# A fused QKV projection: Strassen on pairs of row tiles, and Hopcroft-Kerr on triples in its place

## The chip, the cores and the metric

The kernel runs on one core of a Trainium2 chip. The metric is the device time of one execution in microseconds (us); lower is better. A core has a matrix engine (TensorE, PE in the profile, its weight loads apart as PEld), three engines for elementwise work (VectorE or DVE, ScalarE or ACT, GpSimd or POOL) and queues that issue DMAs, here mostly that of SyncE (SP). Each engine works through its own queue in order; engines wait for each other through semaphores. Matmuls write PSUM, which has 8 banks of 512 f32 columns; all else lies in SBUF.

## The reference

```python
batch, seq, hidden = 16, 512, 768
qkv = np.matmul(x, w_qkv)            # (16, 512, 768) @ (768, 2304), f32
q, k, v = (qkv[..., n * hidden:(n + 1) * hidden] for n in range(3))
return np.stack([q, k, v], axis=0).astype(np.float32)
```

So it is one product of an 8192 x 768 matrix with a 768 x 2304 matrix, written as three outputs. In row tiles of 128 rows there are 64 tiles; the inner dimension is 6 chunks of 128.

## The kernel before

Everything is ordered by hand (`manual_schedule`, L57): each engine's queue is the order in which the program text issues its instructions. The inner dimension is cut into two halves of 3 chunks, and x is taken in pairs of row tiles (256 rows, 32 pairs). The 2304 columns are cut in two units `q` = 0, 1 of 2 x 512 columns and a remainder `REM` of 256 columns between them.

*Start.* The first three pairs are computed directly, in bf16, while the weights arrive. `load_rows` (DMA at L141) brings rows as they lie, `cast_rows` and `turn_rows` round and transpose them, the latter by TensorE transposes (L167) and copies from PSUM (L145, L147). `block` (L385) runs the chains of six matmuls of 512 columns, with copies out on ACT (L394). Meanwhile DVE casts weights and makes the weight sums of the fast scheme (`sum_w`, L113; a last cast L456), each a 128 x 1536 operation.

*Steady part.* Each of the other 29 pairs goes through `two` (the last through `last`). A pair and a unit are a 2 x 2 by 2 x 2 block product, done with 7 block products instead of 8 (`product`, L212: three matmuls of 512 columns each). Products 1 and 2 are bf16, the other five are f32r (recorded as f32), with operands that are sums. `do` issues one product and what follows it: a copy from a PSUM bank to the output tile by ACT (L226, L233, L239, L243) or an add of a bank to the output tile by DVE (L230, L240, L246; one operand in SBUF, one in PSUM). Sums that several outputs share are not formed anew: the next product accumulates in the same bank. The 256 remaining columns are done directly (`rem_row`, L262; copy L272).

*x for the next pair.* `load_x` (L126) loads x in four DMAs two pairs ahead, two issued by SP and two by ACT. `transpose` (L130, DVE) transposes 32 x 32 blocks of 128 x 1536. POOL rounds to bf16 (`round_x`, L175) and makes four sums and a copy (`sums_x`, L183 to L187; 128 x 384 each). `early` puts this behind the pair's first products.

*Stores.* `store_quad` (L253 to L258) issues on SP two stores per unit, of both row tiles at once, and `rem` one (L273).

The order of products in `two` is a1 b1, remainder, a2 b2 a6 b6 a5 a7 b5 b7 a4 a3 b4 b3, 42 matmuls of 512 columns and 12 of 256 per pair.

Of the kernel before, what the change touches and what calls it, by code (L numbers as in the profile page):

```python
# [10 lines left out]
def kernel(  # L11
# [19 lines left out]

# [3 lines left out]
    B, T, H = x.shape  # L35
    M = B * T
# [5 lines left out]
    NP = M // (2 * P)  # L42
    CB = 512
    REM = N3 - 4 * CB
    Q_OFF = (0, 2 * CB + REM)
    R_OFF = 2 * CB
# [5 lines left out]
    sub = mybir.AluOpType.subtract  # L52

    x_flat = x.rearrange("b t h -> (b t) h")
    out_flat = out.rearrange("s b t h -> s (b t) h")

    ctx.enter_context(tc.manual_schedule())  # L57

    w_pool = ctx.enter_context(tc.tile_pool(name="w", bufs=1))
    tq_pool = ctx.enter_context(tc.tile_pool(name="tq", bufs=2))  # L60
    bt_pool = ctx.enter_context(tc.tile_pool(name="bt", bufs=1))
    o_pool = ctx.enter_context(tc.tile_pool(name="o", bufs=5))
    st_pool = ctx.enter_context(tc.tile_pool(name="st", bufs=4))
    or_pool = ctx.enter_context(tc.tile_pool(name="or", bufs=2))
    xin_pool = ctx.enter_context(tc.tile_pool(name="xin", bufs=3))
    xf_pool = ctx.enter_context(tc.tile_pool(name="xf", bufs=2))
    xb_pool = ctx.enter_context(tc.tile_pool(name="xb", bufs=4))
    rem_pool = ctx.enter_context(tc.tile_pool(name="rem", bufs=1))
    s_pool = ctx.enter_context(tc.tile_pool(name="s", bufs=2))
    ps_pool = ctx.enter_context(tc.tile_pool(name="ps", bufs=8, space=bass.MemoryType.PSUM))  # L70

    tiny = w_pool.tile([P, 1], fp32, name="tiny")
    eye = w_pool.tile([P, 176], bf16, name="eye")[:, :P]
    w_rem = [w_pool.tile([P, KH, REM], bf16, name="w_rem0"), None]

    b1 = [w_pool.tile([P, KT, CB], bf16, name=f"b1_{q}") for q in range(2)]
    b22 = [w_pool.tile([P, KH, CB], f32r, name=f"b22_{q}") for q in range(2)]
    t_0 = w_pool.tile([P, 4, KH, CB], f32r, name="t_0")  # L80
    w_rem[1] = rem_pool.tile([P, KH, REM], bf16, name="w_rem1")
    ts = [[t_0[:, n] for n in range(4)], None]

    def load_w(dst, j0, nj, off, cols):
        rows = w_qkv.rearrange("(p j) n -> p j n", j=KT)
        nc.sync.dma_start(dst, rows[:, j0:j0 + nj, off:off + cols])

    stage = {}

    def load_blocks(q, c, nj=KH):
        if q == 0:
            t = tq_pool.tile([P, KT, CB], fp32, name="st0", tag="tq")
            for j in range(0, KT, nj):
                load_w(t[:, j:j + nj], j, nj, Q_OFF[q] + c * CB, CB)
            stage[q, 0, c], stage[q, 1, c] = t[:, :KH, :], t[:, KH:, :]
        else:
            for h in range(2):  # L100
                t = st_pool.tile([P, KH, CB], fp32, name="st1", tag="st")
                load_w(t[:], h * KH, KH, Q_OFF[q] + c * CB, CB)
                stage[q, h, c] = t[:]

    def sum_w(q, n):
        t1, t2, t3, t4 = ts[q]
        o, in0, in1 = {
            1: (t1, stage[q, 0, 1], stage[q, 0, 0]),
            2: (t2, stage[q, 1, 1], t1),
            3: (t3, stage[q, 1, 1], stage[q, 0, 1]),  # L110
            4: (t4, stage[q, 1, 0], t2),
        }[n]
        nc.vector.tensor_tensor(o, in0, in1, op=sub)  # L113

    xin, xf, xb, sr = {}, {}, {}, {}

    def load_x(p, other):
        xin[p] = xin_pool.tile([P, 2 * P // G, KC], fp32, name="xin")  # L120
        t = xin[p]
        rows = x_flat[p * 2 * P:(p + 1) * 2 * P, :].rearrange("(g b) k -> b g k", b=G)
        for n in range(2):
            for h in range(2):
                i = 2 * h + n
                (nc.sync, other)[h].dma_start(t[i * G:(i + 1) * G], rows[:, :, i * KC:(i + 1) * KC])  # L126

    def transpose(p):
        t = xf_pool.tile([P, KT, 2 * P], fp32, name="xf")
        nc.vector.transpose(  # L130
            t[:].rearrange("p j (g b) -> p g j b", b=G),
            xin.pop(p)[:].rearrange("p g (a j) -> p g j a", a=G),
        )
        xf[p] = t

    def load_rows(p):
        xin[p] = xin_pool.tile([P, 2, K], fp32, name="xin")
        rows = x_flat[p * 2 * P:(p + 1) * 2 * P, :]  # L140
        nc.sync.dma_start(xin[p][:], rows.rearrange("(r m) k -> m r k", m=P))  # L141

    def copy_halves(dst, src, two):

        nc.vector.tensor_copy(out=dst[0], in_=src[0])  # L145
        if two:
            nc.scalar.activation(dst[1], src[1], ident)  # L147
        else:
            nc.vector.tensor_copy(out=dst[1], in_=src[1])

    xc = {}

    def cast_rows(p, two=True):
        src = xin.pop(p)
        xc[p] = s_pool.tile([P, 2, K], bf16, name="xc", tag="s")
        for r in range(2):
            halves = (slice(0, K // 2), slice(K // 2, K))
            copy_halves([xc[p][:, r, n] for n in halves], [src[:, r, n] for n in halves], two)

    def turn_rows(p, two=True):  # L160
        c = xc.pop(p)
        xb[p] = xb_pool.tile([P, KT, 2 * P], bf16, name="xb", tag="xb")
        for r in range(2):
            cols = c[:, r, :].rearrange("m (p j) -> m j p", j=KT)
            ps = ps_pool.tile([P, KT, P], bf16, name="ps")
            for j in range(KT):
                nc.tensor.transpose(ps[:, j, :], cols[:, j, :], eye)  # L167
            ks = (slice(0, KH), slice(KH, KT))
            copy_halves(
                [xb[p][:, n, r * P:(r + 1) * P] for n in ks], [ps[:, n, :] for n in ks], two  # L170
            )

    def round_x(p):
        xb[p] = xb_pool.tile([P, KT, 2 * P], bf16, name="xb", tag="xb")
        nc.gpsimd.tensor_copy(out=xb[p][:], in_=xf[p][:])  # L175

    def sums_x(p):
        t = xf.pop(p)
        a11, a12 = t[:, :KH, :P], t[:, KH:, :P]
        a21, a22 = t[:, :KH, P:], t[:, KH:, P:]  # L180
        s = s_pool.tile([P, 5, KH, P], f32r, name="s")
        g = nc.gpsimd
        g.tensor_tensor(s[:, 1], a21, a22, op=add)  # L183
        g.tensor_tensor(s[:, 2], s[:, 1], a11, op=sub)  # L184
        g.tensor_tensor(s[:, 3], a11, a21, op=sub)  # L185
        g.tensor_copy(out=s[:, 0], in_=a22)
        g.tensor_tensor(s[:, 4], a12, s[:, 2], op=sub)  # L187
        sr[p] = s


    class Quad:
        pass

    def quad(p, q):
        u = Quad()
        u.p, u.q = p, q
        u.o = o_pool.tile([P, 2, 2 * CB], fp32, name="o", tag="o")
        u.x = u.y = u.z = None
        return u

    def product(u, n, ps, start):
        t1, t2, t3, t4 = ts[u.q]
        if n <= 2:
            h = (n - 1) * KH
            lhs = [xb[u.p][:, h + j, :P] for j in range(KH)]
            rhs = [b1[u.q][:, h + j, :] for j in range(KH)]
        else:
            k, t = {3: (4, b22[u.q][:]), 4: (0, t4), 5: (1, t1), 6: (2, t2), 7: (3, t3)}[n]
            lhs = [sr[u.p][:, k, j, :] for j in range(KH)]
            rhs = [t[:, j, :] for j in range(KH)]  # L210
        for j in range(KH):
            nc.tensor.matmul(  # L212
                ps[:], lhs[j], rhs[j],
                start=(start and j == 0), stop=(j == KH - 1), skip_group_check=True,
            )

    def bank():
        return ps_pool.tile([P, CB], fp32, name="ps")

    def do(u, n):  # L220
        c11, c12 = u.o[:, 0, :CB], u.o[:, 0, CB:]
        c21, c22 = u.o[:, 1, :CB], u.o[:, 1, CB:]
        if n == 1:
            u.x = bank()
            product(u, 1, u.x, True)
            nc.scalar.activation(c11, u.x[:], ident)  # L226
        elif n == 2:
            u.z = bank()
            product(u, 2, u.z, True)
            nc.vector.tensor_tensor(c11, c11, u.z[:], op=add)  # L230
        elif n == 6:
            product(u, 6, u.x, False)
            nc.scalar.activation(c12, u.x[:], ident)  # L233
        elif n == 5:
            u.y = bank()
            product(u, 5, u.y, True)
        elif n == 7:
            product(u, 7, u.x, False)
            nc.scalar.activation(c22, u.x[:], ident)  # L239
            nc.vector.tensor_tensor(c22, c22, u.y[:], op=add)  # L240
        elif n == 4:
# [182 lines left out]
    for j in range(2, KT):  # L424
        cast_k(j)
# [75 lines left out]
```

## Time and profile before

| what | value |
|---|---|
| timed runs, median (lowest to highest of 3) | 363.17 us (363.01 to 363.24) |
| profiled execution, span from first to last instruction | 361.3 us |
| TensorE matmul | 353.4 us busy, 1765 recorded |
| TensorE weight load | 251.0 us busy |
| DVE | 224.4 us busy |
| ACT | 182.9 us busy |
| POOL | 173.9 us busy |
| DMA | 108.08 MB, 299 GB/s on average; SP's queue 80.8%, ACT's 9.6% of the 16 engines' time |
| granted TensorE clock | 1.000 |

The page gives no other time of the profiled execution than its span; the timed runs are other executions of the same program, 1.8 us longer than the span. Busy time of TensorE is not a rate: the records of successive matmuls overlap, so the distance between their starts is what one costs. The same holds for DVE and ACT where nothing is waited for: the next instruction starts about 0.08 (DVE) or 0.10 us (ACT) before the record of the one ahead of it ends. A line such as `L240 DVE TENSOR_TENSOR o<-o,ps 128x512 f32 ... x58 | 39.9, 688 | 91.2 <-ACT` names the source line, the engine, the tiles written and read, their shape, the count, the busy us in all, the mean ns of one, and the idle us ahead of it with what ended the wait.

### The profile page before, as it was taken

The page shows a single profiled execution, that of the slowest core. Times are in us where ns is not written, and L with a number is a line of the kernel's source. Part 1 is how long each engine was busy: PE and PEld are TensorE (multiplying, and loading weights), DVE is VectorE, ACT ScalarE, POOL GpSimd, SP SyncE. Part 2 cuts the span into 40 slices and gives each one's busy share as a digit, 9 for nine tenths or more (in the row PEclk, how much of TensorE's full clock was granted, in tenths as well). Part 3 has the DMA queues.
Part 4 walks back from the last instruction along what each step waited for, and adds up shares of the span by engine and source line. Part 5 has one row for each costly group of instructions (what it writes and reads, how often), then busy time and mean ns, then how long its engine had stood idle before and what let it go on. Part 6 is the DMA issues. An engine that isn't in the chain of part 4 may idle for free.

```text
span 361.3 us, 5221 instructions
## 1 busy us (share of the span) xinstructions
PE 353.4 (98%) x1765; PEld 251.0 (69%) x1797; DVE 224.4 (62%) x239; ACT 182.9 (51%) x304; POOL 173.9 (48%) x180
## 2 busy tenths in 40 slices
PE   8999999999999999999999999999999999999995
PEld 3644577777777777777777777777777777777763
DVE  3499826765566765566675565676556676556642
ACT  4547555455454545454545445455545454545452
POOL 0001861746664445664445665444665444666410
PEclk9999999999999999999999999999999999999999
DMA  7999869988898999899899999998989899999666
GB/s 298 405 388 373 286 221 359 331 289 295 278 328 301 294 273 294 276 324 315 280 280 290 281 308 309 291 289 278 292 288 321 295 300 271 297 272 339 264 261 232
DMA packets 80617, 108.08 MB, mean 299 GB/s; under 512 B 4816, under 2 KB 60368, under 8 KB 80592
## 3 DMA queue, kind: packets, MB, share of 16 engines
q1 hardware_dynamic: 65184, 96.35, 80.8%
q10 hardware_dynamic: 15408, 11.41, 9.6%
q8 instruction: 14, 0.23, 0.3%
q14 instruction: 11, 0.09, 0.1%
HBM read 32.24 MB, written 75.50 MB: 298 GB/s over the span
## 4 chain that ended last, share of the span: by engine, by line
PE 96%; ACT 1%; issue 1%; ACTq 0%; DVE 0%
PE ps L212 75%; PE ps L262 11%; PE ps L385 9%; PE ps L365 1%; PE ps L167 1%; ACT o L243 0%; ACTq L303 0%; ACT xb L147 0%; ACT orem L317 0%; DVE xb L145 0%; ACT xc L147 0%; ACTq L319 0%; DVE zero L346 0%; ACTq L317 0%
## 5 line engine op out<-in xcount | busy, mean ns | idle before, releaser
L212 PE MATMUL ps<-t,s 128*128 128x512 f32 x696 | 173.8, 398 | 0.0
L212 PEld LDWEIGHTS ps<-t,s 128*128 128x128 f32 x696 | 130.7, 188 | 29.7
L175 POOL CAST xb<-xf 128x1536 bf16<-128x1536 f32 x29 | 43.8, 1510 | 168.3 <-DVE xf L130 156.0
L240 DVE TENSOR_TENSOR o<-o,ps 128x512 f32<-128x512 f32 x58 | 39.9, 688 | 91.2 <-ACT o L239 91.2
L130 DVE STREAM_TRANSPOSE xf<-xin 128x1536 f32<-128x1536 f32 x29 | 85.5, 2950 | 3.7 <-DMA out_dram<-orem 2.1
L212 PE MATMUL ps<-b,xb 128*128 128x512 bf16 x320 | 82.4, 380 | 1.5
L239 ACT ACTIVATE o<-ps 128x512 f32<-128x512 f32 x58 | 34.8, 600 | 44.2 <-PE ps L212 44.2
L212 PEld LDWEIGHTS <-xb 128*128 128x128 bf16 x348 | 31.7, 98 | 35.6 <-issue 7.3
L233 ACT ACTIVATE o<-ps 128x512 f32<-128x512 f32 x58 | 34.9, 601 | 42.1 <-PE ps L212 39.4
L246 DVE TENSOR_TENSOR o<-o,ps 128x512 f32<-128x512 f32 x58 | 39.9, 688 | 21.3 <-PE ps L212 20.2
L212 PE MATMUL ps<-b,s 128*128 128x512 f32 x174 | 48.7, 389 | 0.0
L262 PE MATMUL ps<-w_rem,xb 128*128 128x256 bf16 x384 | 47.2, 273 | 0.0
L243 ACT ACTIVATE o<-ps 128x512 f32<-128x512 f32 x58 | 34.7, 599 | 24.1 <-PE ps L212 21.3
L226 ACT ACTIVATE o<-ps 128x512 f32<-128x512 f32 x58 | 34.7, 598 | 23.8 <-DVE o L246 20.6
L262 PEld LDWEIGHTS <-xb 128*128 128x128 bf16 x384 | 37.4, 98 | 11.2 <-issue 0.5
L230 DVE TENSOR_TENSOR o<-o,ps 128x512 f32<-128x512 f32 x58 | 36.5, 673 | 5.4 <-PE ps L212 4.1
L212 PEld LDWEIGHTS ps<-b,s 128*128 128x128 f32 x174 | 32.7, 188 | 6.8
L184 POOL TENSOR_TENSOR s<-s,xf 128x384 fp32r<-128x384 f32 x29 | 30.0, 1035 | 2.3
L183 POOL TENSOR_TENSOR s<-xf 128x384 fp32r<-128x384 f32 x29 | 30.9, 1064 | 0.0
L185 POOL TENSOR_TENSOR s<-xf 128x384 fp32r<-128x384 f32 x29 | 29.5, 1017 | 0.0
L187 POOL TENSOR_TENSOR s<-xf,s 128x384 fp32r<-128x384 f32 x29 | 29.5, 1016 | 0.0
L272 ACT ACTIVATE orem<-ps 128x512 f32<-128x512 f32 x31 | 18.5, 598 | 20.7 <-PE ps L262 19.5
(36 smaller groups left out, 129.4 us busy)
## 6 DMA issues: line engine op xcount, KB each, us to landing
out_dram<-o SPq DMA_DIRECT2D x62, 768.0 KB, 4.8
out_dram<-o SPq DMA_DIRECT2D x65, 256.0 KB, 4.1
xin<-in_x_dram SPq DMA_DIRECT2D x62, 192.0 KB, 6.9
xin<-in_x_dram ACTq DMA_DIRECT2D x54, 192.0 KB, 4.4
out_dram<-orem SPq DMA_DIRECT2D x31, 256.0 KB, 5.7
st<-in_w_qkv_dram SPq DMA_DIRECT2D x6, 768.0 KB, 13.1
xin<-in_x_dram SPq DMA_DIRECT2D x3, 768.0 KB, 5.7
st<-in_w_qkv_dram SPq DMA_DIRECT2D x6, 256.0 KB, 6.1
```

Of the source, the lines that this page charges most:

```text
L130: nc.vector.transpose(t[:].rearrange("p j (g b) -> p g j b", b=G), xin.pop(p)[:].rearrange("p g (a j) -> p g j a", a=G),)
L175: nc.gpsimd.tensor_copy(out=xb[p][:], in_=xf[p][:])
L212: nc.tensor.matmul(ps[:], lhs[j], rhs[j], start=(start and j == 0), stop=(j == KH - 1), skip_group_check=True,)
L226: nc.scalar.activation(c11, u.x[:], ident)
L230: nc.vector.tensor_tensor(c11, c11, u.z[:], op=add)
L233: nc.scalar.activation(c12, u.x[:], ident)
L239: nc.scalar.activation(c22, u.x[:], ident)
L240: nc.vector.tensor_tensor(c22, c22, u.y[:], op=add)
L243: nc.scalar.activation(c21, u.x[:], ident)
L246: nc.vector.tensor_tensor(c12, c12, u.y[:], op=add)
L262: nc.tensor.matmul(ps, xb[p][:, j, r * P:(r + 1) * P], w_rem[j // KH][:, j % KH, :], start=(j == 0), stop=(j == KT - 1), skip_group_check= ...
L385: nc.tensor.matmul(ps[n][:], xb[p][:, j, r * P:(r + 1) * P], w[:, j, :], start=(j == 0), stop=(j == KT - 1), skip_group_check=True,)
```

## The change

The kernel is rewritten around triples of row tiles. Seven row tiles (`ND`) are computed directly in bf16, in groups of six matmuls of 384 columns (`HC`, half of q, k or v). The other 57 form 19 triples. Rows i = 1, 2, 3 of a triple have two halves of the inner dimension, x_i and y_i; the weights have the halves u_c and v_c for c = 1, 2, 3 (q, k, v). A triple times the weights is a 3 x 2 by 2 x 3 block product, done by 15 block products instead of 18, for each half of 384 columns (`Half`, `run`). A block product is three matmuls of 384 columns. 13 of the 15 are f32r with operands that are sums; C and C' are bf16.

Six PSUM banks (12, 31, 32, 23, 13, 21; 31 and 32 alternate between two banks each) hold running chains. A chain may be *seeded*: ACT or DVE writes its first value into PSUM and matmuls accumulate on top. Per half, ACT seeds 31 and 13 from ta (the copy of product A) and DVE seeds 21, 32 and 23 from ta, e12 and e31 (SBUF copies made by ACT). Three products of a half (N7, Q7, Q6) run within the next half.

x for the next triple: three block transposes on DVE (`first`, `between`), two roundings and two negations on ACT (`late_1`), eleven sums on POOL (four behind the third transpose, one in `late_1`, six at the triple's end). All loads and stores are issued by SP; a store is one row tile's 384 columns. Weight sums: M6 and M7 on POOL, A and B' on ACT, the others on DVE, in tiles of 128 x 2304. The core of the diff:

```diff
-    o_pool = ctx.enter_context(tc.tile_pool(name="o", bufs=5))
+    t_pool = ctx.enter_context(tc.tile_pool(name="t", bufs=13))
+    s_pool = ctx.enter_context(tc.tile_pool(name="s", bufs=16))
+    x_pool = ctx.enter_context(tc.tile_pool(name="x", bufs=8))
+    c_pool = ctx.enter_context(tc.tile_pool(name="c", bufs=15))
+    e_pool = ctx.enter_context(tc.tile_pool(name="e", bufs=5))
...
+        def sum_x(self, name):
+            (x1, y1), (x2, y2), (x3, y3) = (self.xy(i) for i in range(3))
+            s, g = s_tile(f32r), self.s
+            a, b, op = {
+                "A": lambda: (x1, y1, add),
+                "M1": lambda: (x2, y1, add),
+                "B'": lambda: (x2, y2, add),
+                "N1": lambda: (g["A"][:], x3, sub),
+                "Q1": lambda: (g["B'"][:], y3, sub),
+                "M6": lambda: (x1, x2, sub),
+                "M7": lambda: (y2, y1, sub),
+                "N6": lambda: (x3, x1, sub),
+                "N7": lambda: (y3, g["N1"][:], sub),
+                "Q7": lambda: (y3, y2, sub),
+                "Q6": lambda: (x3, g["Q1"][:], sub),
+            }[name]()
+            two(pool, s[:], a, b, op)
...
+        for j in range(KH):
+            pe.matmul(
+                ps[:, :HC], lhs[:, j, :], rhs[:, j0 + j, h * HC:(h + 1) * HC],
                 start=(start and j == 0), stop=(j == KH - 1), skip_group_check=True,
             )
...
+    def run(H_, prev, first, between, late):
+        u = H_.u
+        H_.mul("A", "12", True)
+        ta = e_tile()
+        H_.keep(ta[:], H_.read("12"))
+        first()
+        if prev:
+            prev.mul("N7", "31")
+            prev.mul("Q7", "23")
+        H_.keep(H_.read("31"), ta[:], -1.0)
+        H_.keep(H_.read("13"), ta[:])
+        if prev:
+            prev.end_31()
+        H_.mul("B", "12")
+        e12 = e_tile()
+        H_.keep(e12[:], H_.read("12"))
+        if prev:
+            prev.end_23()
+        two(dve, H_.read("21"), ta[:], e12[:], sub)
+        H_.mul("C", "31")
+        e31 = e_tile()
+        H_.keep(e31[:], H_.read("31"))
+        two(dve, H_.read("32"), e31[:], ta[:], add)
+        dve.scalar_tensor_tensor(H_.read("23"), e31[:], -1.0, e12[:], mult, sub)
+        H_.mul("A'", "13")
+        c11 = H_.take("13", 1, 1, -1.0)
+        if prev:
+            prev.mul("Q6", "32")
+            prev.end_32()
+        H_.mul("M1", "12")
+        c21 = c_tile()
+        two(dve, c21[:], c11[:], H_.read("12"), add)
+        between()
+        H_.mul("B'", "21")
+        c22 = H_.take("21", 2, 2, -1.0)
+        H_.mul("N1", "31")
+        late()
+        H_.mul("C'", "32")
+        c33 = H_.take("32", 3, 3, -1.0)
+        H_.mul("Q1", "23")
+        H_.c32 = c_tile()
+        two(dve, H_.c32[:], c22[:], H_.read("23"), add)
+        c13 = c_tile()
+        two(dve, c13[:], c33[:], H_.read("31"), add)
+        H_.mul("M6", "12")
+        H_.take("12", 1, 2)
+        H_.mul("M7", "21")
+        two(dve, c21[:], c21[:], H_.read("21"), add)
+        H_.out(2, 1, c21)
+        H_.mul("N6", "13")
+        two(dve, c13[:], c13[:], H_.read("13"), add)
+        H_.out(1, 3, c13)
...
+    sum_w("A'", dve, u1, v1, sub)
+    minus_w("A", u1)
+    for h in range(2):
+        for r in range(4, ND):
+            group(r, 0, h, wq)
+    for h, engines in ((0, (dve, act)), (1, (dve, dve))):
+        cut = slice(h * HC, (h + 1) * HC)
+        for k, (eng, t) in enumerate(zip(engines, (u2, v2))):
+            copy(eng, wk[:, k * KH:(k + 1) * KH, cut], t[:, :, cut])
+    sum_w("M6", pool, u1, u2, add)
+    sum_w("M7", pool, v1, v2, add)
+    sum_w("B", dve, u2, v2, sub)
+    sum_w("M1", dve, u1, v2, add)
...
+    sum_v3("N7", v1, v3, add)
+    transpose(ND)
+    transpose(ND + 1)
+    minus_w("B'", v2)
...
+    sum_w("Q6", dve, u3, u2, add)
+    sum_v3("N1", v3, T["A'"], sub)
+    transpose(ND + 2)
+    for name in ALL[:4]:
+        t0.sum_x(name)
...
+    sum_w("Q1", dve, u3, T["B"], add)
+    sum_w("N6", dve, T["N1"], u3, sub)
+    for r in range(ND):
+        group(r, 2, 0, wv)
+    sum_v3("Q7", T["Q1"], v3, sub)
...
+        def first_1():
+            if nxt:
+                transpose(r1 + 2)
+                for name in ALL[:4]:
+                    nxt.sum_x(name)
...
+        def late_1():
+            if nxt:
+                nxt.round_x("B")
+                nxt.round_x("A'")
+                nxt.sum_x("Q1")
+                nxt.minus_x(0)
+                nxt.minus_x(1)
+
+        half = Half(u, 0, n)
+        run(half, prev, first_0, between_0, late_0)
+        prev, n = half, n + 1
+        half = Half(u, 1, n)
+        run(half, prev, first_1, nothing, late_1)
+        prev, n = half, n + 1
+        if nxt:
+            for name in ALL[5:]:
+                nxt.sum_x(name)
+            nxt.drop()
```

`first_0` and `between_0` each transpose one row tile of the next triple. `two` is a tensor_tensor of the engine named; `keep` is an ACT copy with a scale, `take` an ACT copy into an output tile with its store, `end_31`, `end_23` and `end_32` finish an output of the half before.

## The prediction

> **What bounds the kernel now.** I read the busy shares, then the chain that ended last, then the timelines of single engines. All times are microseconds from the span's start unless they are marked ns.
>
> The page's busy line and its chain by engine:
>
> ```profile
> PE 353.4 (98%) x1765; PEld 251.0 (69%) x1797; DVE 224.4 (62%) x239; ACT 182.9 (51%) x304; POOL 173.9 (48%) x180
> ...
> PE 96%; ACT 1%; issue 1%; ACTq 0%; DVE 0%
> ```
>
> TensorE is the bound: the chain is 96% matmul, and the others have room. The chain in order of time gives the rhythm:
>
> ```profile
> 44.12 1.31 PE ps L262 x12
> 45.43 1.30 PE ps L212 x6
> 46.73 1.31 PE ps L262 x12
> ...
> 57.47 1.31 PE ps L262 x12
> ```
>
> One pair of row tiles takes 57.47 - 46.73 = 10.74. So the span is 9.3 to the first chained matmul, 36.1 of direct work up to 45.4, 29 pairs at 10.74 (311.5, to 357.0) and 4.4 behind the last matmul: 361.3. The timed runs' median is 363.17; the 1.8 lies outside the first and last instruction, and I carry it over.
>
> What one matmul costs, from TensorE's timeline:
>
> ```profile
> 107.66 0.84 PE L212 MATMUL ps<-b,s 128*128 128x512 f32 x3
> 108.34 0.84 PE L212 MATMUL ps<-t,s 128*128 128x512 f32 x3
> 109.02 0.84 PE L212 MATMUL ps<-b,s 128*128 128x512 f32 x3
> 109.70 1.47 PE L212 MATMUL ps<-b,xb 128*128 128x512 bf16 x6
> ```
>
> Starts count, not durations: three 512-column f32 matmuls start 0.68 apart, 226.7 ns each. The bf16 ones start 216 ns apart, and the twelve of 256 columns above take 1.31, 109.2 ns each. Half way between, bf16 at 384 columns is 162.5 ns. f32 at 384 is not in the trace: if its 10.9 ns over bf16 is a fixed cost, 173.4 ns; if it goes with the columns, 170; if its weight load (188 ns in the page's groups) could not overlap the next, 188. I take 173.4: with bf16, two matmuls of 256 columns cost 2.4 ns more than one of 512, so a fixed part per matmul is what the rows show. That loads overlap shows in the transposes, which start 56 ns apart with loads recorded at 125.
>
> **The new matmuls.** Direct: 7 row tiles x 36 x 162.5 = 41.0, and 18 transposes x 56 ns = 1.0. A triple has 2 halves x 15 products x 3 matmuls, 78 f32 and 12 bf16: 78 x 173.4 + 12 x 162.5 = 15.48. A pass from f32 to bf16 and back costs some 40 ns now (10.74 less its matmuls), and a triple has four: 15.64. The pair's rate is 16.11 for three row tiles, so TensorE alone gains: 9.3 + 42.0 + 19 x 15.64 + 4.6 (as now, and 0.2 more for a DVE add behind the last product) = 353.1, 8.2 less than now.
>
> **Whether the other engines keep up.** Their costs, from the groups of the page and those by form:
>
> ```profile
> L130 DVE STREAM_TRANSPOSE xf<-xin 128x1536 f32<-128x1536 f32 x29 | 85.5, 2950 | 3.7 <-DMA out_dram<-orem 2.1
> L240 DVE TENSOR_TENSOR o<-o,ps 128x512 f32<-128x512 f32 x58 | 39.9, 688 | 91.2 <-ACT o L239 91.2
> L226 ACT ACTIVATE o<-ps 128x512 f32<-128x512 f32 x58 | 34.7, 598 | 23.8 <-DVE o L246 20.6
> L183 POOL TENSOR_TENSOR s<-xf 128x384 fp32r<-128x384 f32 x29 | 30.9, 1064 | 0.0
> ```
>
> At 384 columns: ACT 0.49 (between 385 ns for 256 and 598 for 512), 0.39 to the next when nothing is waited for (512 columns: 0.494); DVE 0.56 (688 less 128 columns), 0.43 to the next (two L230 start 0.562 apart); a transpose of one row tile 1.43; a POOL sum 0.97 to the next. Writes into PSUM by ACT or DVE and the scalar_tensor_tensor are in no row; the same operations into SBUF are the nearest, I take those, 0.13 either way. From a product's end to its reader's start: 0.2 to 0.25.
>
> I follow one half (`run`) in its queues, from the start of A. TensorE would need 7.74. ACT: ta done 1.26, -ta into 31 at 1.80, ta into 13 at 2.2, end_31 2.6, e12 3.0, end_23 3.4, e31 3.8. DVE: the seed of 21 may begin at 3.02 (e12), of 32 at 3.82 (e31), of 23 behind it: done 3.6, 4.4, 4.8. TensorE wants them at 4.13 (B'), 5.17 (C') and 5.66 (Q1). So the seeds come in time, by 0.5 to 0.8. The transposes lie before e12 and behind c21, where DVE is free; the four extra ACT operations of the second half push its last copy to 7.8, which holds up the next A by 0.13 per triple. DVE's backlog of about 1.0 does not grow. Per triple ACT has 26 x 0.4 and DVE 18 x 0.43 + 3 x 1.43 = 12.0 of 15.6. On queues alone the change is hidden.
>
> **What that leaves out.** DVE's and POOL's timelines where the weight sums meet the x sums:
>
> ```profile
> 34.42 1.73 DVE L113 TENSOR_TENSOR t<-st,st 128x1536 fp32r<-128x1536 f32 x1
> 36.05 3.03 DVE L113 TENSOR_TENSOR t<-st,t 128x1536 fp32r<-128x1536 f32 x1
> 39.01 1.75 DVE L456 CAST b<-st 128x1536 fp32r<-128x1536 f32 x1
> ```
>
> ```profile
> 34.68 2.80 POOL L175 CAST xb<-xf 128x1536 bf16<-128x1536 f32 x1 [33.37 <-DVE xf L130]
> 37.45 2.49 POOL L183 TENSOR_TENSOR s<-xf 128x384 fp32r<-128x384 f32 x1
> 40.02 1.59 POOL L184 TENSOR_TENSOR s<-s,xf 128x384 fp32r<-128x384 f32 x1
> 41.57 0.99 POOL L185 TENSOR_TENSOR s<-xf 128x384 fp32r<-128x384 f32 x1
> ```
>
> A sum of two SBUF tiles on DVE (1.75 elsewhere) and POOL's operations (1.46 and 1.0 elsewhere) exclude each other, in turns: POOL's cast waits until 36.05, DVE's sum until 37.45, POOL's sum until 39.0, DVE's cast (0.95 elsewhere) until 39.9. Each takes its own time plus the rest of the other's. DVE's adds with one PSUM operand (L240) stay at 686 to 690 ns beside POOL, and the transposes don't block it. Now the two hardly meet after 41. In the new kernel all three seeds of a half read two SBUF tiles, and POOL has 11 sums per triple, begun behind the third transpose in the second half and lasting into the next first half: it is at work when the seeds of either half come.
>
> The Trainium skill, page "SBUF — State Buffer", section "Who interferes with whom", gives the inputs alone as the reason: a DVE instruction's second SBUF input comes through an interface shared with GpSimd, and the later one waits in full. By it seeds into PSUM wait too (428 below); by the rows read narrowly, which all write SBUF, they don't (375). No run here shows a seed yet.
>
> With turns: the first seed starts at s, between 3.02 and 3.99 (rest of a POOL sum); POOL takes 0.97 between the seeds; 32 starts at s + 1.40, 23 at s + 2.80, done s + 3.36. Q1 begins at s + 3.41 instead of 5.66. DVE's end_32 and c21 follow (s + 4.22), and M6, which overwrites the bank that c21 reads, begins at s + 4.27; three products more: the half ends at s + 5.83, 8.85 to 9.82. Mean 9.33, and 0.1 for N7 behind the previous half's late c13: two halves 18.8 (18 to 19.8) instead of 15.77. POOL is done in 11 x 0.97 + 6 x 0.43 = 13.3.
>
> **Before the triples.** The weight sums M6 and M7 are POOL sums of 2304 columns: 6 x 0.97 = 5.8 at most, 2.7 at least (one sum and the cast's slope, 1.0 per 1152 columns); I take 5.1, the sum's own slope. That M6 starts when `u2` is in, near 20 (6.9 MB of loads ahead of and with it, at the 0.36 to 0.40 MB per us of these stages), as DVE ends A' and turns to wk's casts: the first cast waits for M6, to 27.6, while q's chains end at 24.2: 3.5 (to 8.7 if M6 is ahead of A'). Behind k, DVE has N7, Q6, N1, Q1, N6, Q7 (2.4 to 2.6 each) and three transposes, from Q6 on in turns with POOL's 11 sums: it ends near 69 by addition, and the first seed stands behind it. B' of the first triple, which TensorE could begin near 59, begins near 70.7; its first half lacks POOL in return. I take 10 (5 to 15).
>
> **Sum.** 9.3 + 42.0 + 3.5 + 10 + 19 x 18.8 (357.2) + 4.6 = 426.6; with 1.8, **428**.
>
> **Rivals.**
> Only what writes SBUF excludes POOL (prologue alone): 353.1 + 2.5 (19 x 0.13) + 1 (first half's bare chain) + 1 (loads) + 13.5 + 1.8 = 373 to 375.
> Seeds collide in one half alone, because POOL drifts clear of the other: a triple 17.2, total 398.
> No blocking that counts: seeds and prologue slip through, TensorE stays the bound, 353.1 + 4.5 + 1.8 = 359.4 (354 with 170 ns). For it speaks that each queue has room; against it the rows above. It decides below 3.8 of blocking in all, 0.2 per triple; from there the change is slower.
> SP issues 30 DMAs per triple. Stores of 128 rows cost about 0.35 and 0.05 between, some 13 in all, hidden; at the 0.77 median of x loads, 24.6, over 470 in all. The bytes are the same, so I hold this unlikely.
> Weight loads at 188 ns add 0.5 per triple to the forecast (437), or 22 to the unblocked case.
>
> **Chances.** Forecast 0.60, one half 0.13, prologue alone 0.10, no blocking 0.13, SP or more 0.04. Range 372 to 450: it leaves out the unblocked case and SP. Faster by over 0.2% (what a measurement of this kernel can tell) 0.12, within 0.02, slower 0.86.
>
> **What would show it.** Right: the seeds' DVE rows at 1.0 to 1.6 instead of 0.56, POOL's sums above 1.0, TensorE idle ahead of Q1 and M6 behind DVE, 18 to 20 between triples, f32 matmuls starting 170 to 174 ns apart inside a product. Wrong: seeds at 0.56 beside a busy POOL, or TensorE dense at 15.7 per triple.

## The result, and the profile after

The changed kernel takes 396.86 us (median of 5 runs, 395.24 to 397.31) against 363.01 for the kernel before: a ratio of 1.0931, 95% interval 1.0910 to 1.0951. It is slower, inside the stated range, by 34 us where the forecast had 65. The profiled execution took 395.2 us with a span of 393.2, so 2.0 lie around the span.

In the changed kernel all sums go through one helper, so most rows have line L146 (`two`); they are told apart by tiles: `b` is a PSUM bank, `e` the SBUF copies ta, e12 and e31, `c` an output tile, `s` a sum of x, `x` a transposed x, `t` weights. From the busy line and the groups:

```profile
PE 366.8 (93%) x2019; PEld 301.3 (77%) x2019; DVE 344.7 (88%) x459; ACT 247.7 (63%) x553; POOL 246.7 (63%) x217
...
L146 POOL TENSOR_TENSOR s<-x 128x384 fp32r<-128x384 f32 x133 | 149.5, 1141 | 77.1 <-DVE x L133 69.1
...
L146 DVE TENSOR_TENSOR c<-c,b 128x384 f32<-128x384 f32 x228 | 115.5, 545 | 9.7 <-PE b L219 6.0
...
L146 DVE TENSOR_TENSOR b<-e 128x384 f32<-128x384 f32 x76 | 63.0, 835 | 23.4 <-ACT e L241 22.4
...
L289 DVE SCALAR_TENSOR_TENSOR b<-e 128x384 f32<-128x384 f32 x38 | 35.0, 920 | 0.0
```

DVE's adds with one PSUM operand (`c<-c,b`) cost 545 ns, where 560 had been worked out. The seeds (`b<-e`, two SBUF operands; L289 is seed 23) are as long in columns and cost 835 and 920 ns. POOL's sums are longer than their 1.0 us too. That is what the forecast's mutual exclusion would look like, now on instructions that write PSUM; e1, e2 and f2 below test it.

DVE's timeline in one triple of the steady part (a first half from 202.8, a second from 210.8):

```profile
203.47 1.65 DVE L133 STREAM_TRANSPOSE x<-x 128x768 f32<-128x768 f32 x1
205.77 0.57 DVE L146 TENSOR_TENSOR b<-e 128x384 f32<-128x384 f32 x1 [0.66 <-ACT e L241]
206.53 1.09 DVE L146 TENSOR_TENSOR b<-e 128x384 f32<-128x384 f32 x1 [0.19 <-ACT e L241]
207.54 0.55 DVE L289 SCALAR_TENSOR_TENSOR b<-e 128x384 f32<-128x384 f32 x1
...
208.94 1.61 DVE L133 STREAM_TRANSPOSE x<-x 128x768 f32<-128x768 f32 x1
...
212.29 1.60 DVE L133 STREAM_TRANSPOSE x<-x 128x768 f32<-128x768 f32 x1
213.95 0.57 DVE L146 TENSOR_TENSOR b<-e 128x384 f32<-128x384 f32 x1
214.72 1.08 DVE L146 TENSOR_TENSOR b<-e 128x384 f32<-128x384 f32 x1 [0.20 <-ACT e L241]
215.72 1.37 DVE L289 SCALAR_TENSOR_TENSOR b<-e 128x384 f32<-128x384 f32 x1
```

and POOL's, of the same stretch:

```profile
204.88 1.00 POOL L146 TENSOR_TENSOR s<-x,s 128x384 fp32r<-128x384 f32 x1
205.85 1.34 POOL L146 TENSOR_TENSOR s<-x 128x384 fp32r<-128x384 f32 x1
210.69 1.99 POOL L146 TENSOR_TENSOR s<-x 128x384 fp32r<-128x384 f32 x2 [3.49 <-DVE x L133]
214.06 1.32 POOL L146 TENSOR_TENSOR s<-s,x 128x384 fp32r<-128x384 f32 x1 [1.39 <-PE b L219]
215.60 1.06 POOL L146 TENSOR_TENSOR s<-s,x 128x384 fp32r<-128x384 f32 x1 [0.23 <-PE b L219]
```

In the first half only seed 32 meets a sum: POOL's started at 205.85, waited for seed 21 and ended at 207.19, and seed 32 took 1.09. Then POOL has nothing to do until 210.69, and seed 23 is free. In the second half 32 waits for the sum of 214.06, 23 for that of 215.60. Over the 17 triples in between, the first halves last 8.08 us on average (8.00 to 8.53) and the second 8.94 (8.76 to 9.00). The last triple prepares no x for a next one: it has no transposes, and no sum meets its seeds. Its halves last 7.774 and 7.773, where TensorE was said to need 7.74. So the profile itself holds the undisturbed rate.

Before the triples, DVE and POOL:

```profile
20.82 2.55 DVE L146 TENSOR_TENSOR t<-t 128x2304 fp32r<-128x2304 f32 x1
23.28 11.98 DVE L94 CAST t<-t 128x1152 bf16<-128x1152 f32 x3
35.19 5.01 DVE L146 TENSOR_TENSOR t<-t 128x2304 fp32r<-128x2304 f32 x2
```

```profile
21.80 11.79 POOL L146 TENSOR_TENSOR t<-t 128x2304 fp32r<-128x2304 f32 x2 [20.50 <-DMA t<-in_w_qkv_dram]
```

Three casts of k's weights take 12 us beside POOL's two weight sums (5.80, 5.40 and 0.94 one by one). TensorE's two large waits, from its timeline:

```profile
29.14 2.08 PE L383 MATMUL b<-t,xb 128*128 128x384 bf16 x6 [3.05 <-DVE t L94]
```

```profile
60.94 1.35 PE L219 MATMUL b<-t,s 128*128 128x384 f32 x6
70.10 2.26 PE L219 MATMUL b<-t,s 128*128 128x384 f32 x6 [7.80 <-DVE b L146]
```

The first is the wait for the first cast of wk (a hole of 3.4 between starts), the second B' of the first triple waiting for its seed, which stands on DVE behind the last weight sums (a hole of 8.1). The first half of the first triple lasts 17.5.

### The profile page after: what moved, and what is told of

The parts are those of the page before. It is cut to its first block, busy times and chain, and to the rows that moved or that the text cites. A ratio compares the mean times of both kernels' runs of the same rounds, so it can differ in the third digit from the quotient of the medians.

```text
span 393.2 us, 7231 instructions
## 1 busy us (share of the span) xinstructions
PE 366.8 (93%) x2019; PEld 301.3 (77%) x2019; DVE 344.7 (88%) x459; ACT 247.7 (63%) x553; POOL 246.7 (63%) x217
## 5 line engine op out<-in xcount | busy, mean ns | idle before, releaser
L219 PE MATMUL b<-t,s 128*128 128x384 f32 x1482 | 294.7, 346 | 16.0 <-DVE b L146 8.4
L219 PEld LDWEIGHTS b<-t,s 128*128 128x128 f32 x1482 | 255.5, 189 | 42.7 <-issue 19.1
L146 POOL TENSOR_TENSOR s<-x 128x384 fp32r<-128x384 f32 x133 | 149.5, 1141 | 77.1 <-DVE x L133 69.1
L241 ACT ACTIVATE c<-b 128x384 f32<-128x384 f32 x228 | 111.7, 491 | 75.8 <-PE b L219 74.2
L146 DVE TENSOR_TENSOR c<-c,b 128x384 f32<-128x384 f32 x228 | 115.5, 545 | 9.7 <-PE b L219 6.0
L133 DVE STREAM_TRANSPOSE x<-x 128x768 f32<-128x768 f32 x57 | 92.4, 1623 | 0.0
L146 DVE TENSOR_TENSOR b<-e 128x384 f32<-128x384 f32 x76 | 63.0, 835 | 23.4 <-ACT e L241 22.4
L241 ACT ACTIVATE e<-b 128x384 f32<-128x384 f32 x114 | 56.2, 493 | 40.9 <-PE b L219 39.8
L146 POOL TENSOR_TENSOR s<-s,x 128x384 fp32r<-128x384 f32 x38 | 49.4, 1301 | 30.6 <-PE b L219 22.9
L219 PE MATMUL b<-wv,sb 128*128 128x384 bf16 x228 | 50.9, 332 | 0.0
L146 POOL TENSOR_TENSOR s<-x,s 128x384 fp32r<-128x384 f32 x38 | 39.0, 1027 | 0.0
L289 DVE SCALAR_TENSOR_TENSOR b<-e 128x384 f32<-128x384 f32 x38 | 35.0, 920 | 0.0
L92 ACT ACTIVATE c<-b 128x384 f32<-128x384 f32 x42 | 19.2, 491 | 16.0 <-PE b L383 13.7
L146 POOL TENSOR_TENSOR t<-t 128x2304 fp32r<-128x2304 f32 x2 | 11.8, 5916 | 20.5 <-DMA t<-in_w_qkv_dram 20.5
L204 ACT ACTIVATE sb<-x 128x384 bf16<-128x384 f32 x38 | 17.6, 511 | 0.0
L146 DVE TENSOR_TENSOR t<-t 128x2304 fp32r<-128x2304 f32 x6 | 16.2, 2732 | 0.0
```

The source lines that it names most:

```text
L92: act.activation(o, i, ident)
L133: dve.transpose(t[:].rearrange("p j (g b) -> p g j b", b=G), xin.pop(r)[:].rearrange("p g (a j) -> p g j a", a=G),)
L146: eng.tensor_tensor(o, a, b, op=op)
L204: act.activation(self.sb[:, k], self.xy(2)[1 - k], ident, scale=-1.0)
L219: pe.matmul(ps[:, :HC], lhs[:, j, :], rhs[:, j0 + j, h * HC:(h + 1) * HC], start=(start and j == 0), stop=(j == KH - 1), skip_group_check= ...
L241: act.activation(o, i, ident, scale=scale)
```

## The experiments

Each was timed in turns with the kernel before on the same chip, whose median was 362.6 to 362.7 us in each set. "First gap" is the hole ahead of the first triple's seeds; halves and triples are means of the 17 triples in between (the first and the last left out), read from the starts of the matmuls of one profiled execution. That of e3 is the slowest of its four runs (421.16).

| run | us | ratio to before (95%) | first A at | first half | halves | triple |
|---|---|---|---|---|---|---|
| changed kernel | 396.86 | 1.0931 (1.0910 to 1.0951) | 57.8 | 17.5 | 8.08, 8.94 | 17.02 |
| e1 | 384.18 | 1.0593 (1.0578 to 1.0609) | 56.5 | 21.0 | 8.13, 8.05 | 16.18 |
| e2 | 376.26 | 1.0373 (1.0343 to 1.0404) | 56.9 | 20.8 | 7.89, 7.84 | 15.73 |
| e3 | 416.63 | 1.1514 (1.1445 to 1.1583) | 59.2 | 17.5 | 9.20, 9.07 | 18.27 |
| e4 | 390.94 | 1.0765 (1.0730 to 1.0799) | 56.3 | 14.2 | 8.17, 8.89 | 17.06 |
| e5 | 396.18 | 1.0918 (1.0900 to 1.0937) | 56.5 | 20.4 | 8.64, 8.29 | 16.93 |
| e6 | 390.42 | 1.0762 (1.0746 to 1.0778) | 54.0 | 18.2 | 8.64, 8.30 | 16.93 |
| e7 | 390.09 | 1.0756 (1.0738 to 1.0774) | 52.7 | 17.6 | 8.62, 8.31 | 16.93 |
| e9 | 392.31 | 1.0813 (1.0794 to 1.0832) | 54.5 | 19.0 | 8.05, 8.95 | 17.00 |
| f2 | 379.19 | 1.0478 (1.0440 to 1.0516) | 58.1 | 19.8 | 7.93, 7.94 | 15.87 |
| f1 | 367.80 | 1.0135 (1.0115 to 1.0156) | 53.7 | 8.5 | 7.94, 7.95 | 15.89 |
| f3 | 369.07 | 1.0173 (1.0159 to 1.0188) | 53.5 | 9.4 | 7.92, 7.85 | 15.76 |

The code ahead of the triples is the same in the changed kernel, e1, e2, e3, e5 and f2. Their first A still comes anywhere from 56.5 to 59.2, so smaller differences in that column say nothing.

### e1: seeds from PSUM

```diff
-        two(dve, H_.read("21"), ta[:], e12[:], sub)
+        two(dve, H_.read("21"), ta[:], H_.read("12"), sub)
...
-        two(dve, H_.read("32"), e31[:], ta[:], add)
-        dve.scalar_tensor_tensor(H_.read("23"), e31[:], -1.0, e12[:], mult, sub)
+        two(dve, H_.read("32"), ta[:], H_.read("31"), add)
+        dve.scalar_tensor_tensor(H_.read("23"), H_.read("31"), -1.0, e12[:], mult, sub)
```

> Change: the three seeds take one operand from the PSUM bank that still holds it (21 = ta - bank 12, 32 = ta + bank 31, 23 = -bank 31 - e12) instead of from its SBUF copy; ACT still makes the copies. Theory (DVE instructions with two SBUF inputs and POOL's sums exclude each other, and this is what lengthens a triple from 15.7 to 16.96 us): seeds at 0.55 us each, POOL sums at 1.0, a triple at 15.7 to 15.8, so about 17 x 1.2 = 20 us less: 375 to 378 us. Rival (DVE and ACT queues are simply fuller with transposes, roundings and negations, and the seeds' long records only show waiting): a triple stays above 16.7, 393 to 397 us.

Measured: 384.18. The seeds fell to 562 and 558 ns. The triple fell from 17.02 to 16.18, two thirds of what was expected, while the first triple's gap grew from 8.1 to 11.4 (why, see "What stays open"). The theory of the port has the larger part; neither theory named the rest. Its groups show where it sits:

```profile
L146 DVE TENSOR_TENSOR b<-e,b 128x384 f32<-128x384 f32 x76 | 42.6, 562 | 28.9 <-ACT e L241 28.9
L289 DVE SCALAR_TENSOR_TENSOR b<-b,e 128x384 f32<-128x384 f32 x38 | 21.2, 558 | 0.0
```

Seeds 21 and 32 wait 28.9 us in all for ACT's copies e12 and e31, though they no longer read them: both engines read the same bank, and in the trace DVE's read stands behind ACT's. It is not the load of transposes or sums: e1's last triple, which prepares no x, has halves of 8.14 and 8.05 too, where the changed kernel's has 7.77.

### e2: no sums on POOL

```diff
         def sum_x(self, name):
+            if self.r0 > ND:
+                self.s[name] = t0.s[name]
+                return
```

(and roundings in tiles of their own, two tiles fewer for the sums). Later triples multiply the first triple's sums, so this kernel leaves out part of the work.

> Change: POOL makes its eleven sums for the first triple alone and the later triples reuse them (the output of later triples is left wrong in this); transposes, roundings, negations, seeds and all matmuls stay; roundings get tiles of their own. Theory of the port: seeds at 0.55 us with unchanged seeds, triple 15.7 to 15.8, 375 to 378 us. Rival of the full queues: triple above 16.7, 393 to 397 us.

Measured: 376.26, triple 15.73. The seeds were left as they were, and so were DVE's transposes and ACT's roundings:

```profile
L147 DVE TENSOR_TENSOR b<-e 128x384 f32<-128x384 f32 x76 | 43.0, 566 | 22.9 <-ACT e L245 22.9
L293 DVE SCALAR_TENSOR_TENSOR b<-e 128x384 f32<-128x384 f32 x38 | 21.3, 560 | 0.0
```

Two SBUF inputs cost nothing extra while POOL is silent. The rival of the full queues is refuted: with them unchanged, a triple has 0.18 over the 15.55 of the last triple.

### e3: all sums behind the third transpose

```diff
                 transpose(r1 + 2)
+                pool.tensor_copy(out=after3[:], in_=xf[r1 + 2][:, 0, :1])
                 for name in ALL[:4]:
```

> Change: a POOL copy of one column of the third transpose's result stands ahead of the eleven sums, so that all of them start behind the third transpose, as the prediction had it. If the prediction's walk by turns was right and only the start of POOL's sums was misplaced: a triple at 18 to 19 us, 17 x 1.0 to 2.0 more, 414 to 432 us, and seeds of both halves at about 1.0 or more. If the turns cost less than the walk says whatever the order: a triple below 17.5, under 406 us.

Measured: 416.63, triple 18.27, seeds at 977 (21 and 32) and 1325 ns (23); only seed 21 of the second halves stayed at 0.57. This is the order in which the forecast had placed POOL's work, and it gives nearly the forecast's triple (18.8). The one-column copy takes 0.6 us of POOL itself.

### e4 and e9: the prologue

e4:

```diff
-    for h, engines in ((0, (dve, act)), (1, (dve, dve))):
+    for h, engines in ((0, (act, act)), (1, (act, act))):
...
-    sum_w("M6", pool, u1, u2, add)
-    sum_w("M7", pool, v1, v2, add)
+    sum_w("M6", dve, u1, u2, add)
+    sum_w("M7", dve, v1, v2, add)
```

> Change: before the triples alone: the four casts of k's weights go to ACT, the weight sums M6 and M7 from POOL to DVE. Theory (in turns with POOL's 5.9 us sums DVE's casts take 5.8 and 5.4 us instead of 0.75, TensorE waits 3.4 us for them, and the first triple's seeds stand behind DVE's late sums): no 3.4 us gap near 26 us, the first triple's 8.1 and 1.6 us gaps smaller by some us, 383 to 392 us, a triple unchanged at 16.96. Rival (DVE's load alone makes the late start): two more sums on DVE, 5 us, come straight on top, 396 us or more.

Measured: 390.94. That is in the theory's range. The first half of the first triple fell from 17.5 to 14.2, its gap from 8.1 to 4.8; that its first A came 1.5 earlier is within the scatter. The hole near 26 did not vanish, it became 2.0 and 0.7: on ACT the casts stood behind the copies of q's last chains, so another queue held them, not turns with POOL.

e9 moves the two weight sums alone:

> Change against the kernel after: only the weight sums M6 and M7 go from POOL to DVE; all casts stay where they are. Theory of turns: DVE's casts at 0.75 us, the 3.4 us gap near 26 falls below 1; DVE has 5 us more of sums but no longer waits 9 to 10 us for POOL's two, so the first triple's gap falls too: 387 to 392 us. Rival (DVE's load counts, not the turns): 5 us more, 400 us or more.

Measured: 392.31. DVE's timeline:

```profile
23.42 2.67 DVE L94 CAST t<-t 128x1152 bf16<-128x1152 f32 x3
26.01 9.95 DVE L146 TENSOR_TENSOR t<-t 128x2304 fp32r<-128x2304 f32 x4
```

Three casts take 2.67 instead of 11.98. With five more microseconds of sums on DVE the kernel is faster, which refutes the rival. The theory had only part of it: the hole near 26 fell to 1.5, not below 1, the first gap stayed (8.4 after 8.1), and the time lies 0.3 above its range.

### e5, e6, e7: two of three seeds

e5 takes 32 and 23 from bank 31 and leaves seed 21, which had hardly been blocked (0.57 in every second half, 0.70 on average in the first halves), as it was:

```diff
-        e31 = e_tile()
-        H_.keep(e31[:], H_.read("31"))
-        two(dve, H_.read("32"), e31[:], ta[:], add)
-        dve.scalar_tensor_tensor(H_.read("23"), e31[:], -1.0, e12[:], mult, sub)
+        two(dve, H_.read("32"), ta[:], H_.read("31"), add)
+        dve.scalar_tensor_tensor(H_.read("23"), H_.read("31"), -1.0, e12[:], mult, sub)
```

> Change against the kernel after: seeds 32 and 23 read bank 31 itself instead of its SBUF copy e31, and ACT's copy e31 is dropped; seed 21 keeps its two SBUF inputs (its records were 0.57 us, unblocked, in the steady part). In the run with all three seeds from PSUM the DVE waited for the ACT copies all the same (28.9 us in all) and halves stayed at 8.04 and 8.13. Theory (that rest is ACT's queue, not the port): without e31 and with 21 as before halves near 7.85, triple 15.7 to 15.8, 374 to 378 us. Rival (the rest is DVE's load): halves stay above 8.0, 382 to 385 us.

Measured: 396.18, no gain to speak of; a miss for both. DVE's timeline, then POOL's:

```profile
206.11 1.43 DVE L146 TENSOR_TENSOR b<-e 128x384 f32<-128x384 f32 x1 [0.65 <-ACT e L241]
207.46 0.55 DVE L146 TENSOR_TENSOR b<-e,b 128x384 f32<-128x384 f32 x1
207.93 0.55 DVE L287 SCALAR_TENSOR_TENSOR b<-b,e 128x384 f32<-128x384 f32 x1
```

```profile
206.11 1.01 POOL L146 TENSOR_TENSOR s<-x 128x384 fp32r<-128x384 f32 x1
```

The sums are back at 1.0, the two changed seeds at 0.55, and the one left is blocked in both halves: 1188 ns on average. Tenths of a microsecond decide it: in the changed kernel seed 21 had started 0.08 and 0.11 us ahead of the sum (205.77 and 213.95 against 205.85 and 214.06), here the sum starts with the seed (206.11) or 0.33 ahead of it (214.46 and 214.79), and all that follows on DVE waits.

e6 adds a prologue without turns, e7 fills TensorE's bare chain as well (the direct chain of row tile 4 behind the first A):

> Change: the seeds of e5 and a prologue without turns: M6 and M7 on DVE, A' ahead of the copies of the turned rows, the casts of k's weights on ACT between q's last groups, v's casts on ACT. Theory (the two places of contention add up and are independent): no gap near 26 us, the first triple's gap under 3 us, then 37 halves of 7.85: 360 to 366 us. Rival (DVE's work before the triples, about 36 us from 20 on, is too much whoever shares the port): the first triple still waits 5 us or more, 367 to 373 us.

> Change: e6, and the last direct chain moved behind the first triple's product A (the bare chain A, B, C leaves TensorE idle for 1.65 us there), and the casts of q's last three chunks divided between DVE and ACT (TensorE waits 1.2 us for them near 15). Theory (TensorE is the bound again, so each gap closed shows in full): 2 us less than e6, 358 to 364 us. Rival (the end of DVE's queue sets the first seeds): within 0.5 us of e6.

Measured: 390.42 and 390.09. The triples are e5's. The hole near 26 is gone and the first A comes at 54.0 and 52.7, yet the first triple still waits 8.0 and 8.5: DVE has the weight sums to make and takes turns with POOL's eleven sums of the first triple on the last of them, so its first seed starts at 65.5 and 64.6, TensorE's first A or not. The rivals of both were right on that point, the theories were not.

### f2, f1, f3: no seed left with two SBUF inputs

f2 takes all three from PSUM (32 and 23 as in e5) and issues 21 ahead of the copy e12:

```diff
+        two(dve, H_.read("21"), ta[:], H_.read("12"), sub)
         e12 = e_tile()
         H_.keep(e12[:], H_.read("12"))
         if prev:
             prev.end_23()
-        two(dve, H_.read("21"), ta[:], e12[:], sub)
```

> Change against the kernel after: the seeds of f1 alone (all three from PSUM, 21 ahead of e12, no e31). Theory (e1's rest of 0.3 to 0.35 us per half over 7.77 is the wait of DVE's seeds for ACT's copies of the same banks): halves 7.85 to 8.0, 377 to 382 us. Rival (it is DVE's load of transposes and adds): halves as in e1, 383 to 385 us.

Measured: 379.19, halves 7.93 and 7.94, as the theory had it. Seeds 21 and 32, which had waited 28.9 us for ACT in e1, wait for TensorE alone:

```profile
L146 DVE TENSOR_TENSOR b<-e,b 128x384 f32<-128x384 f32 x76 | 38.6, 556 | 3.1 <-PE b L219 3.0
L287 DVE SCALAR_TENSOR_TENSOR b<-b,e 128x384 f32<-128x384 f32 x38 | 21.5, 566 | 17.8 <-ACT c L241 17.7
```

Seed 23 still needs the copy e12, and 17.7 us of waiting have moved to it (0.47 each); the halves show that TensorE hardly feels it.

f1 joins this to e7's prologue and mends the first triple's queue: its x is loaded and transposed earlier, and Q7's weight sum and the next triple's first transpose stand behind its seeds.

```diff
     sum_w("A'", dve, u1, v1, sub)
+    for n in range(3):
+        load_x(ND + n)
     for r in range(4, ND):
...
+    transpose(ND + 2)
...
-    sum_v3("Q7", T["Q1"], v3, sub)
...
+            if t == 0:
+                out_direct(4, 2, 1, rest)
+                sum_v3("Q7", T["Q1"], v3, sub, (0,))
+                transpose(r1)
...
```

> Change: all three seeds read PSUM, 21 is issued ahead of the copy e12, no copy e31; the prologue of e7, with the first triple's x loaded and transposed earlier, and the last weight sum (Q7) and the next triple's first transpose put behind the first triple's seeds. Theory (no seed can meet a POOL sum, so the loss can't move to another seed as in e5, and the prologue's gap was DVE's queue): halves 7.85 to 8.0, first triple's gap under 3 us, 362 to 369 us, about the time of the kernel before. Rival (something else than the port sets the halves, as in e1 with 8.04 and 8.13): 368 to 374 us.

Measured: 367.80. TensorE is busy 96% of the span (before: 98%), 100 of 100 us between 100 and 200:

```profile
PE 352.7 (96%) x2019; PEld 301.6 (82%) x2019; DVE 297.4 (81%) x454; ACT 237.4 (65%) x524; POOL 210.9 (58%) x215
```

That is 29 us less than the change as made, and still 1.35% slower than the kernel before. The first gap is gone (0.65 is left), but 5.6 us of holes now lie in the second half of the first triple (13.4 instead of 7.9), where DVE makes up the work put off.

> Change: f1, with POOL's sums made for the first triple alone and reused by the later ones (the output of later triples is left wrong in this). It is the most that the change can bring if nothing contends in the triples: TensorE's floor of 353 us of span plus the rest of the prologue's gaps. Theory: halves 7.8, 358 to 364 us, at best 1% under the kernel before. Rival (f1 already has all of it): within 1 us of f1.

Measured: 369.07, not below f1; a miss. The triples fell as expected (15.76 against 15.89), but its first triple took 24.1 instead of 21.8: the granted clock was 0.58 between 66 and 72 and 0.86 between 72 and 78, where f1 had 1.00, and that ate it. What it does show is that sums on POOL cost f1 no more than 0.13 per triple.

## Why the prediction was right in sign and too large in size

**TensorE's prices held.** Matmuls of 384 columns start 173.4 ns apart (f32; 163 in bf16), so the excess over bf16 is the same 10.9 ns at 384 columns as at 512, and weight loads of 189 ns overlap. A half without disturbance lasts 7.77 against 7.74. By these prices TensorE alone would gain the 8 us of the forecast; no run got there, the best (f1) is 5.1 us slower than the kernel before.

**The mechanism held, on instructions that had not been seen.** Whether seeds into PSUM wait for POOL was open; the groups (835 and 920 ns), e2 (566 and 560 with POOL silent) and e1 and f2 (556 to 566 with one PSUM operand, beside POOL's sums) show that the two SBUF inputs decide, not where the result goes. e2 also spares TensorE any wait for later sums; e1 and f2 do not. The rule of the Trainium skill (page "SBUF — State Buffer", section "Who interferes with whom"), by which the seeds would wait, agrees with 835 against 566 ns. The rival in which only the prologue contends is refuted by e2 and f2; the one in which nothing contends, by all of them. DMA issues were no bound: f1 issues as many, with halves of 7.94 and 7.95.

**The prologue held.** Forecast: wk's first cast delays TensorE by 3.5, B' of the first triple begins at 70.7, its half lasts 19.3. Measured: 3.4, 70.1, 17.5. The first A came at 57.8 instead of 54.8, from two things. k's chains began at 29.1 and not at 27.7, as q's chains ended near 25.9 and not at 24.2. And behind the 3.4 us hole the granted clock stood at 0.50 between 29 and 32: the first twelve matmuls of k started 310 and 285 ns apart (two chains) instead of 162.5, some 1.5 us that the forecast did not have. In e1, e2 and e5 the clock behind the same hole was 1.00.

**The step that failed** is one sentence: POOL has 11 sums per triple, "begun behind the third transpose in the second half". The code queues the first four there only in program order of the text (so "four behind the third transpose", under The change, holds for the text alone); on POOL the sum A needs the first row tile alone, M1 and B' the first two. The first transpose ended at 205.12, and the timelines show A behind it as soon as POOL is through with the sums queued before (205.85), M1 and B' behind the second (210.69, x2), N1 alone behind the third. So three sums leave the queue behind the third transpose. M1 and B' lie where no seed is; what is left of the queue, with the next triple's A behind it, ends at 207.19, before seed 23 of the first half; and seed 21 met a sum in neither half of that triple. Half the collisions of the walk don't occur: 8.08 and 8.94 instead of 9.33 twice. e3 puts the sums where the sentence had them, and the triple goes to 18.27 against 18.8. The rival "seeds collide in one half alone" (17.2 per triple, 398 in all), to which 0.13 had been given, has the size that was measured, 17.02 and 396.9, but not quite the picture: one seed of the first half still collides, and seed 21 of the second does not. The sign did not hang on this step, the size did.

A smaller error: the last triple prepares no x, so it runs undisturbed, in 15.55 and not in 18.8.

In the sum, from the matmuls' starts: first A 3.0 later than forecast, first half 1.9 shorter, the other 37 halves with the last three products 314.3 instead of 347.9, the tail 1.0 shorter: 426.6 + 3.0 - 1.9 - 33.6 - 1.0 = 393.1, the span.

**What stays open.** The first gap is longer in e1, e2 and e5 (10.8 to 11.4 us) than in the changed kernel (8.1), with the same code ahead of it, and the traces show why. Their first A comes 0.9 to 1.3 earlier (the clock, above). Their seed 21 comes 1.3 to 1.8 later, at 70.8 to 71.2 instead of 69.4: six DVE operations of a weight sum near 50 took 4.50 in turns with POOL there, and 2.93 in the changed kernel, where POOL waited instead (two of its sums took 7.00, not 4.4 to 4.5). In e1 another 0.5 is M1, which stands ahead of B' and now waits for seed 21. What makes one or the other go first was not found. f1's holes in the first triple were not closed: without them, from 21.8 to 15.9, it would be 361.9, an estimate by subtraction, about 0.2% under the kernel before. Nor were the 0.17 us closed by which f1's halves exceed 7.77, some 6 us over 37 halves, and nobody tried what of them can be had.

## What to carry to other kernels

When instructions of two engines exclude each other, count not only how full each queue is, but which instructions of one can meet which of the other, and place the helper's work by its data, operand by operand, not by its place in the text. Cure all instructions of a kind: with one of three seeds left, the collision moved to it and the whole gain was lost (396.2 against 396.9). And here an operand that still lay in PSUM was worth more there than its copy in SBUF, if the read was issued ahead of the other engine's copy of the same bank or that copy was dropped (f2, 379.2; with both copies ahead of it, e1, 384.2).

## What the runs showed of the hardware

After TensorE's hole of 8.1 us in the changed kernel the granted clock was 0.53 between 66 and 72 and 0.90 between 72 and 78; with e1's hole of 11.4 us, 0.50 and 0.72. So a long wait is paid again behind it: the six f32 matmuls that start at 70.10 take 2.26 us, where six in f1 take 1.34. The length of one hole does not settle it. Behind the same 3.4 us hole the clock between 29 and 32 was 0.50 in the changed kernel and in f2, 0.76 in e3 and 1.00 in e1, e2 and e5. f1's profiled execution kept 1.000 on average with holes of up to 3.1 us, and f3's fell to 0.58 between 66 and 72 with holes of at most 2.2. What decides was not found.

f32 matmuls start 10.9 ns further apart than bf16 ones at 384 columns as at 512 (173.4 against 162.5, 226.7 against 215.8).

Moving two sums of 5.9 us from POOL to DVE, the fuller engine, made the kernel 4.6 us faster by the medians (e9, 392.3 against 396.9). A DVE sum of that size took 2.5 us, and the three casts that had waited for POOL's sums took 2.67 instead of 11.98.
